# A complex recurrence on VectorE: real and imaginary parts in one operation, decay tables behind the gelu, 16 projection steps moved

## Chip, cores and metric

The kernel runs on one core of a Trainium2 chip. The metric is the time of one execution in microseconds; the profiled execution has its own time, and the profile shows its span from the first instruction to the last.

## What is computed

One layer of a hybrid encoder over two requests, 1024 and 256 tokens of width 1024, 1280 tokens together. An RMS norm is followed by one projection to 5120 columns. Branch A is a bidirectional diagonal state-space recurrence (S5) with a gelu and a gated linear unit; branch B is differential attention with rotary positions. Both are gated, projected, merged under sigmoid gates, projected once more, added to the input and normed. The change touches the recurrence, which is in the reference:

```python
bu = jnp.einsum('ngpc,lgc->nlgp', B_bar, us.astype(jnp.complex64))
a = jnp.broadcast_to(A_bar[:, None], bu.shape)
_, h_f = lax.associative_scan(_scan_combine, (a[0], bu[0]), axis=0)
_, h_b = lax.associative_scan(_scan_combine, (a[1], bu[1]), axis=0, reverse=True)
y = jnp.einsum('gcp,lgp->lgc', C_c[0], h_f) + jnp.einsum('gcp,lgp->lgc', C_c[1], h_b)
```

A_bar and bu are complex; 32 groups of 16 channels have 64 states each, in two directions.

## The kernel before

Time is cut into strands of eight tokens (T = 8), so that a scan runs over J = 160 columns per group (128 of the long request, 32 of the short one). Within a strand the work is done by matrices prepared ahead. The state is rotated by a unit complex factor per column (the table `tb`, real and imaginary), so that the recurrence left over has a real decay: the same decay `rt` for the real and the imaginary part. Partitions 0 to 63 carry the forward direction, 64 to 127 the backward one.

The 32 groups go in eight blocks of four (NB = 4), 640 columns a block. A block b passes three functions (lines 788 to 852):

- `in_mm`: ScalarE writes the decay table `rt` (four activations at line 793, one a group, two buffers). For each half block of two groups TensorE makes the real and the imaginary input products in PSUM (`pr_`, `pi_`, lines 799 and 800). VectorE multiplies them with `tb`: four products of 320 columns (lines 805 to 808), into `bm`, `t1` and `t2`. GpSimd adds `t1` and subtracts `t2` (lines 809 and 810). `t1` and `t2` have one buffer each.
- `scan`: for the real and then the imaginary part a forward scan on partitions 0 to 63 (line 820), a backward one on 64 to 127 (line 821), both over 640 columns, and two memsets (824, 825). Then six VectorE operations of 640 columns rotate back (lines 830 to 835), into `e`.
- `out_mm`: 24 TensorE matmuls (lines 848 to 850) from `e` and the inputs, and a gelu on ScalarE for each half block (line 851).

TensorE's order in this stage is written by hand: PE and SP follow the program. Between the recurrence's matmuls stand projection steps (`fill`). A step is three matmuls (lines 729 to 731) of 424 or 432 columns; eight steps are a chunk, which ScalarE evicts (line 735) and stores by its own DMA queue (line 736); three chunks are a tile of 128 output columns, 24 steps. For each tile a weight is loaded by ScalarE's queue (line 218), cast by ScalarE (line 239) and its remainder taken on GpSimd (line 240, `wl`: the weight split) once a tile two before it is done. There are 24 tiles, 576 steps. S_PRE = 22 steps stand ahead of `in_mm(0)`, S_LEAD = 10 behind it, and in each of the eight blocks S_MID = 13 between `in_mm(b + 1)` and `out_mm(b)` and S_END = 4 behind `out_mm(b)`: 168 in all. Attention takes 288 by its own counts. The 120 left are put in by `fill(1000)` (line 1168) behind the first gated unit and attention's gating (`glu_stage`, `ya_stage`), ahead of the merge: its matmuls (`xb`, line 1081 to 1083) take weights that are cast and split at lines 1074 and 1075. There, and on VectorE, GpSimd and ScalarE everywhere, the order is chosen by a scheduler that models the run at build time.

The loop that sets the order (lines 867 to 889) issues for block b: the loads for later blocks, `scan(b)`, `in_mm(b + 1)`, S_MID steps, `out_mm(b)`, S_END steps.

Of the kernel before, what the change touches and what calls it, by code (L numbers as in the profile page):

```python
# [39 lines left out]
S_PRE, S_LEAD, S_MID, S_END = 22, 10, 13, 4  # L40
# [86 lines left out]
def kernel(  # L127
# [624 lines left out]
    with ExitStack() as p2:  # L752
# [34 lines left out]

        def in_mm(b, tb, wb):
            q, gb = b // 2, (b % 2) * NB
            u = U[q]  # L790
            rt = sp_.tile([128, NB, J], F32, tag="rt", name="rt", bufs=2)
            for g in range(NB):
                A.activation(rt[:, g], rmask, AF.Copy, scale=r8[:, b * NB + g:b * NB + g + 1])
            bm = sp_.tile([128, 2, NB, J], F32, tag="bm", name="bm", bufs=2)
            for h in range(NB // 2):
                pr_ = ps_b.tile([128, 2, J], F32, tag="pr", name="pr")
                pi_ = ps_b.tile([128, 2, J], F32, tag="pi", name="pi")
                for g in range(2):
                    PE.matmul(pr_[:, g], wb[:, 0, 2 * h + g], u[:, gb + 2 * h + g], start=True, stop=True)
                    PE.matmul(pi_[:, g], wb[:, 1, 2 * h + g], u[:, gb + 2 * h + g], start=True, stop=True)  # L800
                t1 = sp_.tile([128, 2, J], F32, tag="t1", name="t1")
                t2 = sp_.tile([128, 2, J], F32, tag="t2", name="t2")
                gsl = slice(2 * h, 2 * h + 2)
                tr_, ti_ = tb[:, 0, gsl], tb[:, 1, gsl]
                V.tensor_tensor(bm[:, 0, gsl], pr_, tr_, op=ALU.mult)
                V.tensor_tensor(t1, pi_, ti_, op=ALU.mult)
                V.tensor_tensor(t2, pr_, ti_, op=ALU.mult)
                V.tensor_tensor(bm[:, 1, gsl], pi_, tr_, op=ALU.mult)
                G.tensor_tensor(bm[:, 0, gsl], bm[:, 0, gsl], t1, op=ALU.add)
                G.tensor_tensor(bm[:, 1, gsl], bm[:, 1, gsl], t2, op=ALU.subtract)  # L810
            return rt, bm

        def scan(b, tb, rt, bm):
            n = NB * J
            z = []
            for r in range(2):
                zz = sp_.tile([128, n + 2], F32, tag=f"z{r}", name=f"z{r}")
                rf = rt.rearrange("p g j -> p (g j)")
                bf = bm[:, r].rearrange("p g j -> p (g j)")
# [3 lines left out]
                zv = zz[:, 1:n + 1].rearrange("p (g j) -> p g j", j=J)  # L823
                V.memset(zv[0:64, :, 0:J:JL], 0.0)
                V.memset(zv[64:128, :, JL - 1:J:JS], 0.0)
                z.append(zv)
            e = sp_.tile([128, 2, NB, J], F32, tag="e", name="e", bufs=2)
            f1 = sp_.tile([128, NB, J], F32, tag="f1", name="f1")
            f2 = sp_.tile([128, NB, J], F32, tag="f2", name="f2")
            V.tensor_tensor(e[:, 0], z[0], tb[:, 0], op=ALU.mult)  # L830
            V.tensor_tensor(f1, z[1], tb[:, 1], op=ALU.mult)
# [26 lines left out]
        with tc.manual_schedule(engines={mybir.EngineType.PE, mybir.EngineType.SP}):  # L858
# [415 lines left out]
```

## Time and profile before

| what | value |
|---|---|
| median of 3 runs | 1108.75 us (1108.33 to 1112.75) |
| profiled execution | 1107.61 us |
| its span | 1105.5 us |
| TensorE matmul busy | 1062.7 us, 96% |
| VectorE busy | 765.3 us, 69% |
| ScalarE busy | 462.9 us, 42% |
| GpSimd busy | 325.3 us, 29% |
| mean granted TensorE clock | 0.992 |

Busy time is what the profile records between an instruction's start and end. Matmul records overlap, so a TensorE that is called busy can still take more work. The chain of work that ended last is followed back from the last instruction, at each step to what released it. In the rows, a number in brackets at the end of a timeline row is the engine's idle time just before and what ended it.

### The profile page before, as it was taken

How to read it: one execution, taken by the hardware profiler on the slowest of the kernel's cores; microseconds unless marked ns; L12 is line 12 of the kernel's file. 1: busy time of each engine (PE TensorE's matmuls, PEld its weight loads, DVE VectorE, ACT ScalarE, POOL GpSimd, SP SyncE). 2: the span in 40 equal slices, each digit the busy share in tenths (PEclk: the TensorE clock that was granted, in tenths of full speed). 3: DMA queues.
4: the chain of work that ended last, by engine and by line, in shares of the span. 5: the costliest groups of instructions: out<-in, count | busy, mean ns of one | idle time of the engine just before them, and what ended most of it. 6: DMA issues, size and time to landing. Idle time of an engine off the chain costs nothing.

```text
span 1105.5 us, 17989 instructions
## 1 busy us (share of the span) xinstructions
PE 1062.7 (96%) x6479; PEld 983.2 (89%) x6479; DVE 765.3 (69%) x1534; ACT 462.9 (42%) x929; POOL 325.3 (29%) x435
## 2 busy tenths in 40 slices
PE   8989999999989899999999999999999999999997
PEld 6868877888979888899999999899999999998997
DVE  7996847877599997577767876876443676666434
ACT  5543322322321212555654664554543455543332
POOL 1619887011234232212312222221240003520032
PEclk9999999999999999999999999999999999999999
DMA  8656454445767667417317316302646974568122
GB/s 244 160 162 218 155 165 164 157 134 192 252 196 225 176 186 202 139 36 198 111 36 208 114 58 174 119 25 80 204 124 197 300 223 112 174 202 259 48 58 95
DMA packets 186154, 173.59 MB, mean 157 GB/s; under 512 B 32721, under 2 KB 161745, under 8 KB 186066
## 3 DMA queue, kind: packets, MB, share of 16 engines
q1 hardware_dynamic: 150736, 144.13, 44.2%
q10 hardware_dynamic: 35330, 28.32, 8.1%
q8 instruction: 51, 0.84, 0.3%
q14 instruction: 37, 0.30, 0.1%
HBM read 113.71 MB, written 58.69 MB: 156 GB/s over the span
## 4 chain that ended last, share of the span: by engine, by line
PE 48%; DVE 19%; DMA 7%; ACT 3%; issue 3%; POOL 2%; SPq 0%; POOLq 0%; ACTq 0%; DVEq 0%
PE mm L729 5%; PE mm L730 5%; PE mm L731 5%; PE xb L1081 3%; PE xb L1082 3%; PE xb L1083 3%; DVE z L821 2%; DVE z L820 2%; PE S L947 2%; PE tr L972 2%; PE S L949 2%; DMA yt<-ya_d 2%; PE tr L1214 2%; PE tr L1215 2%; PE tr L1216 2%
## 5 line engine op out<-in xcount | busy, mean ns | idle before, releaser
L729 PE MATMUL mm<-hTh,wh 128*128 128x424 f32 (+1 forms) x576 | 211.9, 368 | 5.2 <-ACT zo L735 5.0
L731 PE MATMUL mm<-hTh,wl 128*128 128x424 f32 (+1 forms) x576 | 205.8, 357 | 0.0
L730 PE MATMUL mm<-hTl,wh 128*128 128x424 f32 (+1 forms) x576 | 205.4, 357 | 0.0
L729 PEld LDWEIGHTS mm<-hTh,wh 128*128 128x128 f32 x576 | 108.8, 189 | 11.4 <-ACT zo L735 7.0
L730 PEld LDWEIGHTS mm<-hTl,wh 128*128 128x128 f32 x576 | 109.0, 189 | 4.5
L731 PEld LDWEIGHTS mm<-hTh,wl 128*128 128x128 f32 x576 | 108.7, 189 | 3.3
L951 DVE TENSOR_REDUCE mx<-S 128x1 f32<-128x1024 f32 (+1 forms) x80 | 84.3, 1058 | 37.8 <-PE S L949 37.5
L955 ACT ACTIVATE p<-S,mx 128x1024 f32<-128x1024 f32 (+1 forms) x80 | 79.2, 993 | 58.9 <-DVE mx L952 47.1
L240 POOL TENSOR_TENSOR wl<-wst,wh 128x1024 fp32r<-128x1024 f32 x24 | 64.8, 2701 | 127.8 <-ACT wh L239 79.2
L962 POOL TENSOR_SCALAR p<-p,rs 128x1024 f32<-128x1024 f32 (+1 forms) x40 | 41.5, 1037 | 201.3 <-DVE rs L960 195.3
L1214 PE MATMUL tr<-wqh,mh 128*128 128x256 f32 x320 | 89.7, 281 | 2.0 <-DVE o L1218 2.0
L1215 PE MATMUL tr<-wql,mh 128*128 128x256 f32 x320 | 89.2, 279 | 0.0
L1216 PE MATMUL tr<-wqh,ml 128*128 128x256 f32 x320 | 88.9, 279 | 0.0
L246 PE MATMUL mm<-hTh,wh 128*128 128x512 f32 (+1 forms) x192 | 75.0, 391 | 0.0
L247 PE MATMUL mm<-hTl,wh 128*128 128x512 f32 (+1 forms) x192 | 72.6, 378 | 0.0
L248 PE MATMUL mm<-hTh,wl 128*128 128x512 f32 (+1 forms) x192 | 72.5, 378 | 0.0
L1214 PEld LDWEIGHTS tr<-wqh,mh 128*128 128x128 f32 x320 | 60.1, 188 | 2.9 <-DVE o L1218 2.9
L1215 PEld LDWEIGHTS tr<-wql,mh 128*128 128x128 f32 x320 | 60.1, 188 | 0.0
L1216 PEld LDWEIGHTS tr<-wqh,ml 128*128 128x128 f32 x320 | 60.0, 188 | 0.0
L735 ACT COPY zo<-mm 128x424 f32<-128x424 f32 (+1 forms) x72 | 37.0, 514 | 53.0 <-PE mm L731 27.1
L1221 POOL TENSOR_TENSOR o<-o,finB 128x256 f32<-128x256 f32 x30 | 28.2, 943 | 103.5 <-ACT jk L1220 103.5
L976 DVE TENSOR_TENSOR wTl<-tr,wTh 128x512 fp32r<-128x512 f32 (+1 forms) x72 | 46.7, 656 | 14.0 <-ACT wTh L975 12.9
(396 smaller groups left out, 2827.1 us busy)
## 6 DMA issues: line engine op xcount, KB each, us to landing
wst<-in_w_in_dram ACTq DMA_DIRECT2D x24, 512.0 KB, 4.2
wst<-in_w_in_dram SPq DMA_DIRECT2D x16, 512.0 KB, 5.4
wst<-in_w_branch_dram SPq DMA_DIRECT2D x32, 256.0 KB, 4.8
wqs<-in_w_out_dram SPq DMA_DIRECT2D x16, 512.0 KB, 4.1
tt_d<-tt SPq DMA_DIRECT2D x16, 320.0 KB, 3.1
tb<-tt_d SPq DMA_DIRECT2D x8, 640.0 KB, 5.0
zt<-gs_d SPq DMA_DIRECT2D x16, 320.0 KB, 3.9
x<-in_x_sample_dram SPq DMA_DIRECT2D x8, 512.0 KB, 5.5
```

Of the source, the lines that this page charges most:

```text
L240: e.tensor_tensor(lv, st, hv, op=ALU.subtract)
L246: PE.matmul(ps[:, :n], wh[:, k, :], hTh[:, k, c0:c0 + n], start=(k == 0), stop=False)
L247: PE.matmul(ps[:, :n], wh[:, k, :], hTl[:, k, c0:c0 + n], start=False, stop=False)
L248: PE.matmul(ps[:, :n], wl[:, k, :], hTh[:, k, c0:c0 + n], start=False, stop=(k == KD - 1))
L729: PE.matmul(ps[:, :n], wh[:, k, :], hTh[:, k, c0:c0 + n], start=(k == 0), stop=False)
L730: PE.matmul(ps[:, :n], wh[:, k, :], hTl[:, k, c0:c0 + n], start=False, stop=False)
L731: PE.matmul(ps[:, :n], wl[:, k, :], hTh[:, k, c0:c0 + n], start=False, stop=(k == KD - 1))
L951: V.tensor_reduce(mx, S[:, :nk], axis=AX.X, op=ALU.max)
L955: A.activation(p[:, :nk], S[:, :nk], AF.Exp, bias=mx, scale=1.0 / math.sqrt(HD), accum_out=sm[:, t:t + 1])
L1214: PE.matmul(ps[:, :256], mh[:, k, ts_], oh_[:, k], start=(k == 0), stop=False)
L1215: PE.matmul(ps[:, :256], mh[:, k, ts_], ol_[:, k], start=False, stop=False)
L1216: PE.matmul(ps[:, :256], ml[:, k, ts_], oh_[:, k], start=False, stop=(k == 7))
```

## The change

It does four things. Real and imaginary parts share one operation: the PSUM products of a half block lie in one tile `pp_`, one VectorE product with the imaginary table writes `t` and one with the real table writes `bm`, each over 640 columns; the forward and the backward scan each run over 1280 columns, with a decay table that holds the same decay twice; two memsets clear the edges; two products of 1280 columns and an add and a subtract of 640 rotate back. The decay table is made by a function of its own, two blocks ahead of its scan, and placed behind the gelu of block b with `after(sig)`, which queues it behind that instruction on ScalarE; the first two are made ahead of `in_mm(0)`. S_LEAD goes from 10 to 18 and S_MID from 13 to 14: 8 + 8 steps come out of the 120 behind attention.

```diff
-S_PRE, S_LEAD, S_MID, S_END = 22, 10, 13, 4
+S_PRE, S_LEAD, S_MID, S_END = 22, 18, 14, 4
...
+        def decay(b):
+            rt = sp_.tile([128, 2, NB, J], F32, tag="rt", name="rt", bufs=2)
+            for g in range(NB):
+                A.activation(rt[:, :, g], bc(rmask, 1, 2), AF.Copy, scale=r8[:, b * NB + g:b * NB + g + 1])
+            return rt.rearrange("p r g j -> p (r g j)")
+
         def in_mm(b, tb, wb):
...
-            rt = sp_.tile([128, NB, J], F32, tag="rt", name="rt", bufs=2)
-            for g in range(NB):
-                A.activation(rt[:, g], rmask, AF.Copy, scale=r8[:, b * NB + g:b * NB + g + 1])
...
-                pr_ = ps_b.tile([128, 2, J], F32, tag="pr", name="pr")
-                pi_ = ps_b.tile([128, 2, J], F32, tag="pi", name="pi")
+                pp_ = ps_b.tile([128, 2, 512], F32, tag="pp", name="pp")
...
-                V.tensor_tensor(bm[:, 0, gsl], pr_, tr_, op=ALU.mult)
-                V.tensor_tensor(t1, pi_, ti_, op=ALU.mult)
-                V.tensor_tensor(t2, pr_, ti_, op=ALU.mult)
-                V.tensor_tensor(bm[:, 1, gsl], pi_, tr_, op=ALU.mult)
-                G.tensor_tensor(bm[:, 0, gsl], bm[:, 0, gsl], t1, op=ALU.add)
-                G.tensor_tensor(bm[:, 1, gsl], bm[:, 1, gsl], t2, op=ALU.subtract)
+                t = sp_.tile([128, 2, n], F32, tag="t", name="t")
+                V.tensor_tensor(t, pp_[:, :, :n], ti_, op=ALU.mult)
+                V.tensor_tensor(bm[:, :, sl_], pp_[:, :, :n], tr_, op=ALU.mult)
+                G.tensor_tensor(bm[:, 0, sl_], bm[:, 0, sl_], t[:, 1], op=ALU.add)
+                G.tensor_tensor(bm[:, 1, sl_], bm[:, 1, sl_], t[:, 0], op=ALU.subtract)
...
         def scan(b, tb, rt, bm):
-            n = NB * J
...
-                V.tensor_tensor_scan(zz[0:64, 2:n + 2], rf[0:64], bf[0:64], 0.0, ALU.mult, ALU.add)
-                V.tensor_tensor_scan(zz[64:128, 0:n][:, ::-1], rf[64:128, ::-1], bf[64:128, ::-1], 0.0,
-                                     ALU.mult, ALU.add)
...
+            n = 2 * NB * J
+            zz = sp_.tile([128, n + 2], F32, tag="z", name="z")
+            bf = bm.rearrange("p r n -> p (r n)")
+            V.tensor_tensor_scan(zz[0:64, 2:n + 2], rt[0:64], bf[0:64], 0.0, ALU.mult, ALU.add)
+            V.tensor_tensor_scan(zz[64:128, 0:n][:, ::-1], rt[64:128, ::-1], bf[64:128, ::-1], 0.0, ALU.mult, ALU.add)
...
-            V.tensor_tensor(e[:, 0], z[0], tb[:, 0], op=ALU.mult)
-            V.tensor_tensor(f1, z[1], tb[:, 1], op=ALU.mult)
-            V.tensor_tensor(e[:, 0], e[:, 0], f1, op=ALU.subtract)
-            V.tensor_tensor(e[:, 1], z[1], tb[:, 0], op=ALU.mult)
-            V.tensor_tensor(f2, z[0], tb[:, 1], op=ALU.mult)
-            V.tensor_tensor(e[:, 1], e[:, 1], f2, op=ALU.add)
-            return e
+            V.tensor_tensor(e, z, tr_, op=ALU.mult)
+            V.tensor_tensor(f, z, ti_, op=ALU.mult)
+            V.tensor_tensor(e[:, 0], e[:, 0], f[:, 1], op=ALU.subtract)
+            V.tensor_tensor(e[:, 1], e[:, 1], f[:, 0], op=ALU.add)
+            return e.rearrange("p r (g j) -> p r g j", j=J)
...
+            rts = [decay(0), decay(1)]
             cur = in_mm(0, tbs[0], wbs.pop(0))
...
                 sig = out_mm(b, wcs.pop(b), e)
+                if b + 2 < NBLK:
+                    with after(sig):
+                        rts.append(decay(b + 2))
                 fill(S_END)
```

In the new code `tr_` and `ti_` are the tables broadcast over the two parts, n is 320 in `in_mm`, and `sl_` is the half block's 320 columns.

## Rows read from the trace of the kernel before

**Rows 1.** The page, chain that ended last: shares of the span by engine.

```profile
PE 48%; DVE 19%; DMA 7%; ACT 3%; issue 3%; POOL 2%; SPq 0%; POOLq 0%; ACTq 0%; DVEq 0%
```

**Rows 2.** Recurrence stage: length, busy PE, PEld, DVE, ACT, POOL (count), clock, DMA share, GB/s.

```profile
290.00:441.00 151.00, 139.63 (x792) 134.11 (x791) 130.84 (x176) 33.46 (x76) 46.73 (x38) 0.98 0.71 206
```

**Rows 3.** VectorE's waits in that stage: waiter, releaser, total us, times, longest.

```profile
DVE z L820 <- POOL bm L809: 2.3, 7, 0.3
DVE t L806 <- POOL bm L809: 1.8, 7, 0.3
```

**Rows 4.** From the first product of block 0 to the end of block 7.

```profile
298.90:436.90 138.00, 126.68 (x715) 121.28 (x713) 130.84 (x176) 28.36 (x62) 46.73 (x38) 0.98 0.70 199
```

**Rows 5.** TensorE's timeline: output matmuls of blocks 0, 1, 2 and 7; an eviction wait.

```profile
319.93 0.83 PE L848 MATMUL tr<-e,wcm 128*128 128x160 f32 x2 [4.55 <-DVE e L832]
...
337.35 0.43 PE L848 MATMUL tr<-e,wcm 128*128 128x160 f32 x2
...
352.68 0.44 PE L848 MATMUL tr<-e,wcm 128*128 128x160 f32 x2
...
365.62 0.46 PE L729 MATMUL mm<-hTh,wh 128*128 128x424 f32 x1 [2.11 <-ACT zo L735]
...
436.26 0.51 PE L848 MATMUL tr<-e,wcm 128*128 128x160 f32 x2 [1.29 <-issue]
```

**Rows 6.** VectorE's timeline: first part of block 3 and its first two scans.

```profile
350.42 0.49 DVE L805 TENSOR_TENSOR bm<-pr,tb 128x320 f32<-128x320 f32 x1
350.82 0.48 DVE L807 TENSOR_TENSOR t<-pr,tb 128x320 f32<-128x320 f32 x1
351.22 0.48 DVE L806 TENSOR_TENSOR t<-pi,tb 128x320 f32<-128x320 f32 x1
...
352.01 0.48 DVE L805 TENSOR_TENSOR bm<-pr,tb 128x320 f32<-128x320 f32 x1
352.75 0.49 DVE L806 TENSOR_TENSOR t<-pi,tb 128x320 f32<-128x320 f32 x1 [0.26 <-POOL bm L809]
...
354.39 2.13 DVE L820 TENSOR_TENSOR_SCAN z<-rt,bm 64x640 f32<-64x640 f32 x1 [0.33 <-POOL bm L809]
356.56 3.51 DVE L821 TENSOR_TENSOR_SCAN z<-rt,bm 64x640 f32<-64x640 f32 x1
```

**Rows 7.** VectorE's timeline: scans and combination of block 2.

```profile
338.77 2.13 DVE L820 TENSOR_TENSOR_SCAN z<-rt,bm 64x640 f32<-64x640 f32 x1 [0.33 <-POOL bm L809]
...
343.96 1.49 DVE L821 TENSOR_TENSOR_SCAN z<-rt,bm 64x640 f32<-64x640 f32 x1
...
346.00 0.83 DVE L830 TENSOR_TENSOR e<-z,tb 128x640 f32<-128x640 f32 x1
346.74 0.82 DVE L834 TENSOR_TENSOR f<-z,tb 128x640 f32<-128x640 f32 x1
```

**Rows 8.** Weight splits on GpSimd, 298.8 to 437: busy us, mean ns, idle before; one split.

```profile
L240 POOL TENSOR_TENSOR wl<-wst,wh 128x1024 fp32r<-128x1024 f32 x6 | 18.3, 3053 | 20.5 <-ACT wh L239 20.5
...
355.15 3.57 POOL L240 TENSOR_TENSOR wl<-wst,wh 128x1024 fp32r<-128x1024 f32 x1
```

**Rows 9.** GpSimd's timeline: add and subtract of block 3's first half.

```profile
351.84 0.88 POOL L809 TENSOR_TENSOR bm<-bm,t 128x320 f32<-128x320 f32 x1 [12.29 <-DVE t L806]
352.69 0.86 POOL L810 TENSOR_TENSOR bm<-bm,t 128x320 f32<-128x320 f32 x1
```

**Rows 10.** Decay tables on ScalarE, 298.8 to 437: busy us, mean ns, idle before.

```profile
L793 ACT ACTIVATE rt<-rmask,r 128x160 f32<-128x160 f32 x24 | 8.3, 418 | 54.4 <-DVE z L821 54.4
```

**Rows 11.** TensorE's and VectorE's timelines where projection steps end and the merge begins.

```profile
842.01 0.42 PE L1081 MATMUL xb<-ysh,wh 128*128 128x320 f32 x1
...
842.56 0.35 PE L729 MATMUL mm<-hTh,wh 128*128 128x424 f32 x1
...
851.84 0.31 PE L1083 MATMUL xb<-ysh,wl 128*128 128x320 f32 x1
...
841.99 1.23 DVE L1075 TENSOR_TENSOR wl<-wst,wh 128x1024 fp32r<-128x1024 f32 x1
```

More of the change, by code (lines that the diff above doesn't have):

```diff
@@ L790, in in_mm @@
             u = U[q]
-            rt = sp_.tile([128, NB, J], F32, tag="rt", name="rt", bufs=2)
-            for g in range(NB):
-                A.activation(rt[:, g], rmask, AF.Copy, scale=r8[:, b * NB + g:b * NB + g + 1])
-            bm = sp_.tile([128, 2, NB, J], F32, tag="bm", name="bm", bufs=2)
+            bm = sp_.tile([128, 2, NB * J], F32, tag="bm", name="bm", bufs=2)
             for h in range(NB // 2):
-                pr_ = ps_b.tile([128, 2, J], F32, tag="pr", name="pr")
-                pi_ = ps_b.tile([128, 2, J], F32, tag="pi", name="pi")
+                pp_ = ps_b.tile([128, 2, 512], F32, tag="pp", name="pp")
@@ L798, in in_mm @@
                 for g in range(2):
[L799 to L804, printed above, removed]
-                V.tensor_tensor(bm[:, 0, gsl], pr_, tr_, op=ALU.mult)
@@ new lines, in in_mm @@
+                    for r in range(2):
+                        PE.matmul(pp_[:, r, g * J:g * J + J], wb[:, r, 2 * h + g], u[:, gb + 2 * h + g],
+                                  start=True, stop=True)
+                n = 2 * J
+                sl_ = slice(h * n, h * n + n)
+                tr_, ti_ = (bc(tb[:, r, 2 * h:2 * h + 2].rearrange("p g j -> p (g j)"), 1, 2) for r in range(2))
+                t = sp_.tile([128, 2, n], F32, tag="t", name="t")
+                V.tensor_tensor(t, pp_[:, :, :n], ti_, op=ALU.mult)
@@ new lines, in in_mm @@
+                V.tensor_tensor(bm[:, :, sl_], pp_[:, :, :n], tr_, op=ALU.mult)
+                G.tensor_tensor(bm[:, 0, sl_], bm[:, 0, sl_], t[:, 1], op=ALU.add)
+                G.tensor_tensor(bm[:, 1, sl_], bm[:, 1, sl_], t[:, 0], op=ALU.subtract)
+            return bm
+        def scan(b, tb, rt, bm):
+            n = 2 * NB * J
[3 more added lines that the diff above has]
+            V.tensor_tensor_scan(zz[64:128, 0:n][:, ::-1], rt[64:128, ::-1], bf[64:128, ::-1], 0.0, ALU.mult, ALU.add)
+            zv = zz[:, 1:n + 1].rearrange("p (g j) -> p g j", j=J)
+            V.memset(zv[0:64, :, 0:J:JL], 0.0)
+            V.memset(zv[64:128, :, JL - 1:J:JS], 0.0)
+            z = zz[:, 1:n + 1].rearrange("p (r n) -> p r n", r=2)
+            e = sp_.tile([128, 2, NB * J], F32, tag="e", name="e", bufs=2)
+            f = sp_.tile([128, 2, NB * J], F32, tag="f", name="f")
+            tr_, ti_ = (bc(tb[:, r].rearrange("p g j -> p (g j)"), 1, 2) for r in range(2))
+            V.tensor_tensor(e, z, tr_, op=ALU.mult)
[3 more added lines that the diff above has]
+            return e.rearrange("p r (g j) -> p r g j", j=J)
@@ L880 @@
                     store_y(q - 1)
-                e = scan(b, tbs.pop(b), *cur)
+                e = scan(b, tbs.pop(b), rts.pop(0), cur)
                 if b + 1 < NBLK:
```

13 lines of the change are left out of this document (removed).

## The prediction

> **What bounds the kernel now.** I read the busy shares by stage first, then the waits inside the recurrence stage, then one block of that stage instruction by instruction. Over the whole program the chain of work that ended last lies mostly on TensorE, with VectorE second [rows 1]. In the recurrence stage it is VectorE: 130.8 of 151 us busy [rows 2], and all that VectorE waits for there, after one load at the start, is GpSimd, seven times before a scan and seven times before a product, 4.1 us together [rows 3]. The stage lasts 138.0 us from the first product of block 0 to the end of block 7 [rows 4].
>
> TensorE runs beside it and is the engine that waits: 4.55 us before the output matmuls of block 0, about 2 us where an eviction was late, 1.29 us before the outputs of block 7 [rows 5]. So what the stage costs is read from VectorE, and the projection steps are what TensorE does meanwhile.
>
> A block without a disturbance has three parts. From its first product to its first scan 3.97 us: 350.42 to 354.39 [rows 6]. From there to the first product after the memsets 7.23 us: 338.77 to 346.00. From there to the next block's first product 4.42 us: 346.00 to 350.42 [rows 6, 7]. Sum 15.62 us, times eight 125.0 us. The other 13.0 us of the 138.0 belong to the six weight splits that GpSimd runs in that time [rows 8], 2.17 us each. How a split costs VectorE is seen in the second scan of the block: 3.51 us in place of 1.49 [rows 6, 7].
>
> **The merged operations, step by step.** Products of 320 columns start 0.40 us apart (350.42, 350.82) [rows 6], operations of 640 columns 0.74 us apart (346.00, 346.74) [rows 7]: about 0.06 us fixed and 1.06 ns a column. Merging saves 0.06 us for each operation that goes. It also changes who waits.
>
> *First part.* Per half block two products of 640 columns replace four of 320. GpSimd's add and subtract now both read the one buffer t, which has one copy, so the second half's t waits for both; before, t1 waited for the add alone. With the first product at 0, bm of the first half starts at 0.74 and ends at 1.56. GpSimd starts 0.14 us after its last input (351.70 to 351.84), its two operations start 0.85 us apart and the second takes 0.86 [rows 6, 9]: it is done at 3.41. Meanwhile bm of the second half runs, as now the second half's first product is put ahead of the waiting one (352.01 before 352.75) [rows 6]. The second t runs from 3.44 to 4.26, GpSimd's second pair from 4.40 to 6.11, the scan starts at 6.14. Before it needed only the add; now it needs the subtract too. That is 2.17 us more than 3.97. If t goes ahead of bm in the second half, 0.74 more.
>
> *Scans.* Nothing in the trace scans 1280 columns. Two scans of 640 take 2.98 us; if a scan has the fixed 0.14 us by which a recorded operation of 640 columns (0.82) exceeds its columns, one of 1280 takes 2.84. I bound it by 2.70 and 2.98 and take 2.84, which is nearest to how the other operations behave. Two of them, two memsets in place of four and the gaps give 6.0 us, against 7.23. Half of that gain is that the first scan, 2.13 us beside GpSimd's subtract [rows 7], now starts when GpSimd is done.
>
> *Combination.* Two products of 1280 columns at 1.42, a subtract and an add of 640 at 0.74: 4.32, and about 0.1 because the subtract reads what the operation just ahead of it wrote. 4.42, as now.
>
> Sum: 6.14 + 6.0 + 4.42 = 16.56 us a block, 0.94 more than 15.62; eight blocks, 7.5 us more.
>
> **The splits.** A weight tile lasts 24 projection steps, and its successor's split follows its last step. From the first step to block 7's outputs there were 22 + 10 + 8 x 13 + 7 x 4 = 164 steps, six full tiles; now there are 180, seven. One more split at 2.17 us; as VectorE now sits waiting for a fifth of a block, a split falls partly in that time, so seven at about 2.0 against six at 2.17: 1.0 us more. Bounds: no more than now, and 3.05 for the one more (the mean split's whole time on GpSimd) [rows 8].
>
> **The decay tables.** Their activations no longer stand on ScalarE ahead of the scan that frees their buffer, where they held the queue for 54.4 us [rows 10], evictions and weight casts behind them included. The price of that was TensorE waiting about 2 us for an eviction [rows 5]. TensorE had that time to spare, since VectorE set the end, so I cost its end at nothing. Each activation is now twice as wide, four a block; 0.42 us each becomes at most 0.84, so at most 3.4 us a block on an engine busy 33 of 151 us [rows 2, 10]. Behind the gelu of block b they have a block's time until the scan of b + 2. Where the gelu waits for TensorE's outputs, evictions queue behind it as now; the cover is the second projection bank. The eight at the start end some microseconds ahead of the first scan. SP's queue and GpSimd's are passed by nothing of this.
>
> **The 16 steps.** Each step is three matmuls; the 16 steps between 842.56 and 851.84 took 9.28 us, 0.58 a step [rows 11]. In the recurrence stage they are covered: TensorE reaches the outputs of block 0 at 315.4 now (319.93 less 4.55 [rows 5]), with nine steps more at 320.6, while block 0 ends on VectorE at 298.9 + 16.6 + 2.2 = 317.7. Later a block takes TensorE 15.33 us (337.35 to 352.68 [rows 5]) and a step more makes 15.9, under VectorE's 16.56 plus splits. The two evictions, two stores and two thirds of a weight load, cast and split that go with the steps move along; ScalarE and its queue have room, and the split is counted above. At the other end, the steps leave the stretch behind attention. There exactly 16 steps stand after the first merge matmul could start (842.01), and that matmul's third term lacks only the weight split, ready at 843.22 [rows 11]. Without the 16 steps TensorE waits about 0.7 us for it: a gain of 8.6 us, bounds 7 and 9.3.
>
> **Sum.** +7.5 + 1.0 - 8.6 = -0.1 us on the profiled execution's 1107.61, so no change; the median of the three runs is 1108.75, 1.1 above it. I forecast **1108.6 us**. The bounds (scans 2.2 us either way, t ahead of bm 5.9 up, splits 2, tail 1.6 up or 0.7 down) make the forecast's own range about 1103.5 to 1115.
>
> **Rivals.**
>
> *The number of operations decides.* A block goes from 22 VectorE operations to 12. If the waits for GpSimd are hidden, because the scheduler puts the next block's first products among the combination of this one (as it did once, between the scans of blocks 0 and 1), a block is 10 x 0.06 us shorter, 4.8 us over the stage, and TensorE at 15.9 a block keeps up: 1108.75 - 4.8 - 8.6 = 1095.3. For it speaks that the two products of a half need only TensorE's inputs. Against it: in a steady block the products now come strictly behind the combination, and t2 comes ahead of t1 (350.82, 351.22 [rows 6]), the order in which TensorE delivers, so the scheduler believed VectorE to be waiting for TensorE there and had no reason to hoist; eight more steps ahead make TensorE later still in its eyes. This is what the Trainium skill says, VectorE: DVE Perf Modes, Rules for kernel authors, where chained operations are to be reduced in number and semaphores are said to matter little. By that rule the stage shrinks; the rows say that a hand-off to GpSimd and back costs 0.14 + 1.71 us and an operation 0.06, so I give it the smaller chance: 0.22.
>
> *GpSimd's order.* GpSimd runs in order, and a weight split may stand ahead of the adds for which VectorE now waits four times a block. Then VectorE pays the whole split, up to 3.57 us [rows 8], not 2.17; with seven splits 1.4 x 7 = 9.8 us, 1118.4. It decides against the kernel from 0.8 us a split on (5.5 / 7). For it: GpSimd already waited 20.5 us with a split at its head for a cast [rows 8]. Against: none of the products' waits in the trace was longer than 0.3 us [rows 3]. 0.13.
>
> *The tail gives nothing back.* If the chain through the gated unit and attention's gating ends later than now, TensorE waits for it where the 16 steps stood, the gain of 8.6 shrinks and the time is up to 1115, inside the range: 0.05.
>
> **Chances.** Forecast 0.60, operations 0.22, GpSimd's order 0.13, tail 0.05. A measurement of this kernel tells about 0.5%, 5.5 us, from no change. Faster: the operations rival and 0.05 of the forecast, 0.27. Slower: GpSimd's order, and 0.09 from the forecast's and the tail's upper ends, 0.22. Same: 0.51. The range 1096 to 1115 leaves out half of the first rival and most of the second.
>
> **What the changed profile would show.** First part of a block near 6.1 us, with VectorE waiting for GpSimd's subtract twice, about 1.2 and 1.9 us; scans near 2.84; period 16.6, or 18.7 with a split; the stage 146 us long; no wait of TensorE for an eviction, but for e in most blocks; no projection step behind the first merge matmul. A first part under 5 us, or products among the combination, would prove the forecast wrong on the fast side; a split ahead of an add with VectorE waiting over 3 us, on the slow side.

## The result and the profile after

The changed kernel takes **1115.86 us** (median of 16 runs, 1110.88 to 1117.53) against 1108.65 for the kernel before on the same chip: ratio 1.0059, 95% interval 1.0045 to 1.0073. It is slower by about 0.6%. The forecast was 1108.6 us, the range 1096 to 1115; the time lies 0.9 us above the range. The profiled execution took 1115.66 us (span 1113.8), 8.4 us of span more than the one before.

I cut the span at four places that both traces have: VectorE's first product of block 0; the end of its last operation of block 7; the start of the last norm matmul of attention; the start of the last projection step's last matmul. "Attention stage" below is from the second to the third. "Units" is the distance from the first to the last unit's reciprocal in attention, which lies inside it and leaves both edges out.

| stage, us | before | after | difference |
|---|---|---|---|
| ahead of the first product | 298.9 | 298.4 | -0.5 |
| recurrence | 138.0 | 146.7 | +8.7 |
| attention stage | 343.6 | 351.7 | +8.1 |
| to the last projection step | 71.1 | 62.2 | -9.0 |
| to the end | 253.8 | 254.9 | +1.1 |

The forecast had +8.5 for the second line and -8.6 for the fourth. It had no line for attention, and nearly the whole error of its sum lies there: 8.1 us, of which 7.6 are in the units (306.8 and 314.4).

**Recurrence.** The windows view, from the first product to the end of block 7, answers to [rows 4]: busy TensorE, weight loads, VectorE, ScalarE, GpSimd with counts, clock, DMA share, GB/s.

```profile
298.36:445.11 146.75, 135.83 (x766) 129.51 (x764) 115.84 (x96) 34.60 (x66) 45.54 (x39) 0.99 0.70 199
```

VectorE has 96 instructions instead of 176 and 115.8 us of work instead of 130.8, and the stage is longer. Its waits, against [rows 3]:

```profile
DVE z L818 <- POOL bm L811: 16.3, 8, 2.5
DVE t L808 <- DMA tb<-tt_d: 10.3, 1, 10.3
DVE t L808 <- PE tr L845: 7.4, 4, 1.9
DVE t L808 <- POOL bm L811: 5.3, 4, 1.9
```

Where 4.1 us of waiting for GpSimd stood, there are 29.0: 16.3 before the scans, and 12.7 before the second half's t. The third line names TensorE, but GpSimd's subtract is what came last: in block 3 it ends at 355.61, and t starts at 355.64. GpSimd's timeline there:

```profile
354.75 0.86 POOL L811 TENSOR_TENSOR bm<-bm,t 128x320 f32<-128x320 f32 x1
```

VectorE's timeline of block 3, in which no split falls, against [rows 6, 7]:

```profile
352.23 0.82 DVE L808 TENSOR_TENSOR t<-pp,tb 128x640 f32<-128x640 f32 x1
352.97 0.81 DVE L809 TENSOR_TENSOR bm<-pp,tb 128x640 f32<-128x640 f32 x1
355.64 0.82 DVE L808 TENSOR_TENSOR t<-pp,tb 128x640 f32<-128x640 f32 x1 [1.86 <-PE tr L845]
356.38 0.81 DVE L809 TENSOR_TENSOR bm<-pp,tb 128x640 f32<-128x640 f32 x1
359.00 2.82 DVE L818 TENSOR_TENSOR_SCAN z<-rt,bm 64x1280 f32<-64x1280 f32 x1 [1.80 <-POOL bm L811]
...
364.99 1.49 DVE L827 TENSOR_TENSOR e<-z,tb 128x1280 f32<-128x1280 f32 x1
...
369.40 0.82 DVE L808 TENSOR_TENSOR t<-pp,tb 128x640 f32<-128x640 f32 x1
...
393.96 4.98 DVE L818 TENSOR_TENSOR_SCAN z<-rt,bm 64x1280 f32<-64x1280 f32 x1 [1.80 <-POOL bm L811]
```

First part 6.77 us (352.23 to 359.00), scans 5.99, combination 4.41: 17.17 a block. In the second half t stands ahead of bm and holds it back. The last line is a scan beside a weight split: 4.98 instead of 2.82. The splits on GpSimd, against [rows 8]:

```profile
L240 POOL TENSOR_TENSOR wl<-wst,wh 128x1024 fp32r<-128x1024 f32 x7 | 16.7, 2389 | 2.6 <-ACT wh L239 2.6
```

Seven, as forecast. Eight blocks of 17.17 are 137.4. Four of the splits lie beside a scan, which takes 2.0 to 2.2 us longer; three stand between GpSimd's two pairs of a block, and the scan behind them waits about 2.4 us instead of 1.8. That is 10.4 us in all, 1.5 a split. In two blocks (1 and 2) the scheduler put the first half's products among the combination of the block before, and this took some 1.1 us off: the first three blocks last 53.9 us (298.36 to 352.23), where three of 17.17 and their splits would make 55.0. VectorE's timeline where blocks 1 and 2 meet, and the scan of block 4, which waits for a pair behind a split:

```profile
331.84 0.82 DVE L808 TENSOR_TENSOR t<-pp,tb 128x640 f32<-128x640 f32 x1
...
333.31 0.81 DVE L829 TENSOR_TENSOR e<-e,f 128x640 f32<-128x640 f32 x1
...
336.31 0.82 DVE L808 TENSOR_TENSOR t<-pp,tb 128x640 f32<-128x640 f32 x1 [0.77 <-POOL bm L811]
...
376.80 2.82 DVE L818 TENSOR_TENSOR_SCAN z<-rt,bm 64x1280 f32<-64x1280 f32 x1 [2.44 <-POOL bm L811]
```

**Attention.** The windows view over the units (columns as above), first of the kernel before.

```profile
450.60:757.43 306.83, 299.87 (x1767) 279.03 (x1767) 226.76 (x418) 167.75 (x343) 70.20 (x50) 1.00 0.36 105
```

The same view of the changed kernel:

```profile
459.75:774.15 314.40, 303.90 (x1765) 281.15 (x1765) 234.72 (x418) 168.97 (x345) 70.32 (x51) 0.99 0.35 101
```

TensorE's work is the same to two matmul records. It stands idle 10.5 us instead of 7.0, and its matmuls take 4.0 us longer. Before, its longest waits in the units were for the exponentials on ScalarE (who waits, for whom, total, times, longest):

```profile
PE S L947 <- ACT p L955: 4.3, 5, 1.4
```

After:

```profile
PE tr L971 <- DVE mx L951: 6.8, 3, 2.3
...
PE mm L729 <- ACT zo L735: 1.8, 4, 0.4
PE tr L983 <- DVE mx L951: 1.7, 3, 0.6
```

Three waits of 2.3 us, at the start of a head each. The first of them, on GpSimd's timeline:

```profile
539.66 2.51 POOL L240 TENSOR_TENSOR wl<-wst,wh 128x1024 fp32r<-128x1024 f32 x1 [16.56 <-ACT wh L239]
542.15 1.56 POOL L961 TENSOR_SCALAR p<-p,rs 128x1024 f32<-128x1024 f32 x1
```

On VectorE's timeline:

```profile
539.95 2.77 DVE L1016 SCALAR_TENSOR_TENSOR ya<-ya,rr 128x512 f32<-128x512 f32 x1
542.64 0.15 DVE L960 TENSOR_TENSOR rs<-rs,nlam 128x1 f32<-128x1 f32 x1
542.75 1.50 DVE L1017 TENSOR_TENSOR ya<-ya 128x512 f32<-128x512 f32 x1
544.17 1.21 DVE L950 TENSOR_REDUCE mx<-S 128x1 f32<-128x1024 f32 x1
545.31 0.41 DVE L996 TENSOR_TENSOR ya<-ya 128x256 f32<-128x256 f32 x1
545.64 1.27 DVE L962 SCALAR_TENSOR_TENSOR p<-p,rs,p 128x1024 f32<-128x1024 f32 x1
```

And on TensorE's:

```profile
546.97 1.09 PE L971 MATMUL tr<-ident,p 128*128 128x128 f32 x8 [2.26 <-DVE mx L951]
```

A weight split starts on GpSimd while VectorE begins a norm operation of the pair just finished (L1016). That operation takes 2.77 us where its neighbour L1015 took 0.68. Behind it in VectorE's order stand the factors rs, the row maxima and the combination of p (L962), and TensorE's transposes (L971) wait for that p. (Their row names mx L951, which ends 0.01 us after they began; p is done at 546.91.) VectorE has no idle time from 539.22 on, and GpSimd's own share of p (L961), held back behind the split, is done at 543.71, so it is VectorE's time that counts.

A split beside a norm product is not enough, though. The kernel before has such meetings too. VectorE's timeline of it, the first product of a norm, which takes 0.68 us undisturbed:

```profile
501.15 2.87 DVE L1015 TENSOR_TENSOR ya<-ya,rr 128x512 f32<-128x512 f32 x1
```

It happens again at 662.58, and two combinations of p take 3.20 us instead of 1.28; yet behind these four TensorE waits 1.0 us at most at a time. At the start of a head, where the change put the meeting, TensorE had run out of work at 544.71, 2.26 us ahead of its transposes.

The clock follows in two of the three cases: it was granted 0.57 and 0.65 of full speed in the 4 us behind the waits at 629.98 and 714.52, so part of each stretch ran at 1.2 GHz and not 2.4. That is 1.7 and 1.4 us of full-speed time lost, an estimate from the granted clock, and so most of the 4.0 us by which the matmuls took longer. Behind the wait at 546.97 it stayed at 1.00. The windows view of the three stretches:

```profile
547.00:551.00 4.00, 4.00 (x24) 3.77 (x25) 3.95 (x8) 3.79 (x7) 1.13 (x1) 1.00 0.35 95
...
630.00:634.00 4.00, 4.00 (x16) 3.82 (x17) 3.95 (x8) 3.27 (x6) 1.12 (x1) 0.57 0.38 102
...
714.50:718.50 4.00, 3.98 (x18) 3.77 (x19) 3.95 (x9) 3.27 (x6) 1.12 (x1) 0.65 0.35 97
```

**The tail.** TensorE's timeline, against [rows 11]:

```profile
849.42 0.31 PE L1080 MATMUL xb<-ysh,wh 128*128 128x320 f32 x1
...
849.86 0.35 PE L729 MATMUL mm<-hTh,wh 128*128 128x424 f32 x1
...
858.95 0.36 PE L731 MATMUL mm<-hTh,wl 128*128 128x424 f32 x1
859.14 0.31 PE L1082 MATMUL xb<-ysh,wl 128*128 128x320 f32 x1
```

Sixteen steps stand behind the first merge matmul, as before. The 16 that left did so from the stretch ahead of it.

### The profile page after: what moved, and what is told of

The parts are those of the page before. It is cut to its first block, busy times and chain, and to the rows that moved or that the text cites. A ratio compares the mean times of both kernels' runs of the same rounds, so it can differ in the third digit from the quotient of the medians.

```text
span 1113.8 us, 17906 instructions
## 1 busy us (share of the span) xinstructions
PE 1067.5 (96%) x6479; PEld 986.6 (89%) x6479; DVE 759.0 (68%) x1454; ACT 468.7 (42%) x929; POOL 321.2 (29%) x435
## 4 chain that ended last, share of the span: by engine, by line
PE 51%; DVE 15%; DMA 7%; issue 4%; POOL 3%; ACT 2%; SPq 0%; POOLq 0%; ACTq 0%; DVEq 0%
PE mm L729 7%; PE mm L730 7%; PE mm L731 7%; DVE z L818 2%; PE tr L971 2%; PE S L946 2%; PE xb L1080 2%; PE S L948 2%; PE xb L1081 2%; PE xb L1082 2%; DVE z L819 2%; PE mm L247 2%; PE mm L246 2%; PE mm L248 2%; PE tr L1213 2%
## 5 line engine op out<-in xcount | busy, mean ns | idle before, releaser
L961 POOL TENSOR_SCALAR p<-p,rs 128x1024 f32<-128x1024 f32 (+1 forms) x40 | 42.6, 1064 | 209.1 <-DVE rs L959 186.7
L240 POOL TENSOR_TENSOR wl<-wst,wh 128x1024 fp32r<-128x1024 f32 x24 | 58.0, 2418 | 115.2 <-ACT wh L239 95.7
```

The lines of the kernel that those rows point to most:

```text
L240: e.tensor_tensor(lv, st, hv, op=ALU.subtract)
```

## The experiments

Theory P: what costs 8 us in attention is the place at which the weight tiles change there. A tile is 24 steps and a head takes 72, so whatever place the tile's change has in one head it has in all four; 168 and 192 steps ahead of attention are whole numbers of tiles, 184 are 16 steps into one. Rival M: the merged operations cause it, by the later end of the recurrence or another order of work behind it. Theory G, for the recurrence: the price is the hand-off to GpSimd. All results in one table. The stages (us) are those of one profiled execution, which can lie some microseconds off the median; the ratio is to the kernel before on the same chip.

| run | steps | recurrence | attention stage | units | to last step | to end | median, ratio (95%) |
|---|---|---|---|---|---|---|---|
| e1_fill_only | 184 | 139.7 | 351.5 | 314.6 | 62.2 | 255.9 | 1108.28, 0.9995 (0.9979 to 1.0011) |
| e2_merge_only | 168 | 144.1 | 344.3 | 306.0 | 72.3 | 253.4 | 1117.25, 1.0066 (1.0046 to 1.0087) |
| e3_rt_only | 168 | 137.9 | 343.6 | 306.4 | 71.1 | 254.1 | 1106.51, 0.9991 (0.9970 to 1.0013) |
| e4_merge_192 | 192 | 151.2 | 344.2 | 306.4 | 56.7 | 262.2 | 1111.12, 1.0022 (1.0011 to 1.0033) |
| f1_t_two | 184 | 138.8 | 350.3 | 314.7 | 62.2 | 257.9 | 1108.57, 0.9982 (0.9962 to 1.0002) |
| f2_v_adds_168 | 168 | 131.6 | 346.2 | 309.4 | 72.3 | 254.7 | 1104.18, 0.9934 (0.9916 to 0.9953) |
| f3_small_184 | 184 | 146.5 | 339.5 | 303.9 | 62.4 | 257.3 | 1106.34, one run |
| f4_small_168 | 168 | 144.0 | 336.9 | 299.5 | 74.8 | 255.9 | 1109.67, one run |
| g1_bm_first | 184 | 144.3 | 350.1 | 314.4 | 62.2 | 257.8 | 1111.79, 1.0031 (1.0016 to 1.0047) |
| g2_fill_176 | 176 | 136.7 | 359.5 | 313.4 | 66.8 | 255.5 | 1113.72, 1.0057 (1.0036 to 1.0077) |
| g3_v_adds_176 | 176 | 131.1 | 346.1 | 308.9 | 66.8 | 255.5 | 1098.70, 0.9908 (0.9886 to 0.9930) |
| g4_v_adds_192 | 192 | 132.5 | 346.3 | 306.9 | 56.7 | 258.5 | 1093.61, 0.9880 (0.9856 to 0.9903) |
| h1_vsplit_184 | 184 | 146.7 | 341.9 | 304.8 | 61.8 | 255.1 | 1105.47, 0.9974 (0.9958 to 0.9990) |
| h2_vsplit_before | 168 | 138.0 | 339.1 | 307.0 | 71.8 | 256.1 | 1102.30, 0.9952 (0.9933 to 0.9971) |
| h3_vsplit_adds_192 | 192 | 132.5 | 338.9 | 303.8 | 57.6 | 258.4 | 1086.22, 0.9808 (0.9787 to 0.9830) |

### Which part costs what: e1, e2, e3, e4

e1_fill_only: the kernel before, steps alone.

```diff
-S_PRE, S_LEAD, S_MID, S_END = 22, 10, 13, 4
+S_PRE, S_LEAD, S_MID, S_END = 22, 18, 14, 4
```

> The kernel before with S_LEAD 18 and S_MID 14 alone: 184 projection steps in the recurrence, nothing merged, decay tables where they were. Theory P (phase): attention takes three weight tiles a head (72 steps), so a count that is no multiple of 24 shifts casts, splits and evictions against attention's units in every head; attention (first scores to the end of its outputs) goes from 344 us to about 350, the stretch behind it loses 6.5 us, the recurrence has one more split (+2 us): total within 3 us of before. Rival M (the merged order is what lengthens attention): attention stays at 344 and the total falls by 5 to 8 us.

The recurrence is 1.7 us longer than before, attention 351.5 and 314.6, as in the changed kernel, though nothing is merged. The 16 steps alone bring the tail's 9.0 us and lose 7.9 of them in attention: ratio 0.9995. P holds, M falls.

e2_merge_only: the changed kernel, steps as before.

```diff
-S_PRE, S_LEAD, S_MID, S_END = 22, 18, 14, 4
+S_PRE, S_LEAD, S_MID, S_END = 22, 10, 13, 4
```

> The changed kernel with S_LEAD 10 and S_MID 13 back: 168 steps, merged operations and decay tables behind the gelu kept. Theory P: first product to the end of block 7 about 145 us (138 before, 146.7 in the changed kernel, one split less), attention back at about 344 us, the tail as before: total 6 to 8 us above before, about the changed kernel's time. Rival M: attention about 350 us as in the changed kernel, total 12 us or more above before.

Recurrence 6.1 us longer than before, attention within 0.8 us of before; by the medians 0.66% slower. So by the medians the merged operations cost what the whole change costs, and the steps bring nothing. The profiled execution took 1112.01 us, the shortest of the six; where the 5 us up to their median lie is not in its trace.

e3_rt_only: the kernel before with the decay tables two blocks ahead, behind the gelu.

```diff
+        def decay(b):
...
+            rts = [decay(0), decay(1)]
...
+                    with after(sig):
+                        rts.append(decay(b + 2))
```

> The kernel before with the decay tables alone put behind the gelu, 160 columns wide as before. Theory W (VectorE sets the recurrence's end): ScalarE's waits of 54 us go, TensorE's waits for evictions too, and the total stays within 2 us of before. Rival: ScalarE's late evictions cost time after all, and the total falls by 3 us or more.

No stage of the table moves by more than 0.3 us, ratio 0.9991 with 1 inside its interval: nothing, as the forecast costed it.

e4_merge_192: the changed kernel with S_LEAD 26.

```diff
-S_PRE, S_LEAD, S_MID, S_END = 22, 18, 14, 4
+S_PRE, S_LEAD, S_MID, S_END = 22, 26, 14, 4
```

> The changed kernel with S_LEAD 26: 192 steps, again a multiple of 24. Theory P: recurrence 147 to 149 us, attention back at about 344 us, the tail shorter than before by 6 to 9 us: total about 1108 to 1112. Rival M: attention about 350 us, total 1114 to 1118. If it is the number of steps left behind attention, and not the phase, that lengthens attention, it is 350 us or more here.

Attention is back at 344.2 and 306.4 with eight steps more than the change moved: it is not the number that costs. Against the changed kernel the tail gives 5.5 us more, but 7.3 are lost behind the last step (262.2), and the recurrence takes 4.5 more, 151.2 where 147 to 149 were expected. Why was not pursued.

### The recurrence: f1, g1, f2

f1_t_two: the changed kernel, two buffers for t.

```diff
-                t = sp_.tile([128, 2, n], F32, tag="t", name="t")
+                t = sp_.tile([128, 2, n], F32, tag="t", name="t", bufs=2)
```

> The changed kernel with two buffers for t instead of one; nothing else. Theory G (in the recurrence the price is the hand-off to GpSimd: the second half's t waits for GpSimd's subtract of the first half, idle 1.86 us in block 3 of the changed kernel): with a second buffer the four products of a block run 0.74 us apart, GpSimd's two pairs run back to back, and the scan starts about 5.2 us after the first product instead of 6.77. A block falls from 17.2 to about 15.6 us, which is at or under what TensorE needs with 18 steps (15.9); the recurrence from its first product to the end of block 7 takes 134 to 139 us instead of 146.8. Rival W (the wide operations themselves cost more than the narrow ones did, by the tables broadcast over two parts or by the PSUM tile's stride): the first part stays above 6 us and the recurrence at 145 to 148. Theory P (a place in the cycle of 24 projection steps decides the attention stage) expects the attention stage as in the changed kernel, 351 to 352 us, in either case, since 184 steps still stand ahead of it. Total: G and P 1104 to 1109; W 1115 to 1117.

Recurrence 138.8, at the upper end of what G gave; all waits of t for GpSimd are gone; the units stay at 314.7. W, that the wide operations themselves cost more, falls. One buffer cost 8 us. VectorE still waits for GpSimd before each scan, 19.9 us in all, and in two blocks the weight split stood between GpSimd's two pairs, the "GpSimd's order" rival in small: 4.4 us instead of 2.07. VectorE's timeline of f1 in one of them:

```profile
365.85 0.82 DVE L808 TENSOR_TENSOR t<-pp,tb 128x640 f32<-128x640 f32 x1
...
373.27 2.82 DVE L818 TENSOR_TENSOR_SCAN z<-rt,bm 64x1280 f32<-64x1280 f32 x1 [4.41 <-POOL bm L811]
```

g1_bm_first: the changed kernel, the products in the other order.

```diff
-                V.tensor_tensor(t, pp_[:, :, :n], ti_, op=ALU.mult)
                 V.tensor_tensor(bm[:, :, sl_], pp_[:, :, :n], tr_, op=ALU.mult)
+                V.tensor_tensor(t, pp_[:, :, :n], ti_, op=ALU.mult)
```

> The changed kernel with its two input products in the other order: bm first, then t; 184 steps. It is the order on which the forecast's first part of 6.14 us rested. Theory G (hand-off): the second half's bm runs while GpSimd works on the first half, only t waits; first part of a steady block 6.1 to 6.2 us instead of 6.77, and as two blocks of the changed kernel had their first half put among the combination already, the recurrence falls from 146.8 to 141 to 144 us; attention stage 350 to 352; total 1110 to 1114. Rival (VectorE's order in the second half is not what is waited for, GpSimd's two pairs set the scan's start in either order): recurrence 146 to 148, total 1115 to 1117.

VectorE's timeline of g1, first part of a block:

```profile
385.03 0.82 DVE L808 TENSOR_TENSOR bm<-pp,tb 128x640 f32<-128x640 f32 x1
385.76 0.82 DVE L809 TENSOR_TENSOR t<-pp,tb 128x640 f32<-128x640 f32 x1
386.50 0.81 DVE L808 TENSOR_TENSOR bm<-pp,tb 128x640 f32<-128x640 f32 x1
388.44 0.82 DVE L809 TENSOR_TENSOR t<-pp,tb 128x640 f32<-128x640 f32 x1 [1.14 <-POOL bm L811]
391.09 4.97 DVE L818 TENSOR_TENSOR_SCAN z<-rt,bm 64x1280 f32<-64x1280 f32 x1 [1.82 <-POOL bm L811]
```

First part 6.06 us (385.03 to 391.09), against 6.14 in the forecast: its sum was right for the order that it assumed. The recurrence falls by 2.5 us to 144.3, just above the 141 to 144 expected, and by less than eight times the 0.71 us of a first part: a split between GpSimd's pairs cost 1.4 us there (a scan's wait of 3.2 for 1.8, in two blocks) and 0.6 in the changed kernel. The total is 1111.79, inside what G gave and below the rival's.

f2_v_adds_168: add and subtract on VectorE over the whole block, steps as before.

```diff
+            t = sp_.tile([128, 2, NB * J], F32, tag="t", name="t")
...
-                G.tensor_tensor(bm[:, 0, sl_], bm[:, 0, sl_], t[:, 1], op=ALU.add)
-                G.tensor_tensor(bm[:, 1, sl_], bm[:, 1, sl_], t[:, 0], op=ALU.subtract)
+            V.tensor_tensor(bm[:, 0], bm[:, 0], t[:, 1], op=ALU.add)
+            V.tensor_tensor(bm[:, 1], bm[:, 1], t[:, 0], op=ALU.subtract)
```

> The changed kernel with the add and the subtract of the input products on VectorE, one of each over the whole block of 640 columns, and the counts of steps as before (10 and 13, 168 steps). No operation of the recurrence is left on GpSimd but the weight split. Theory G (hand-off to GpSimd is the price): first part of a block about 6 x 0.74 = 4.4 us plus 0.1 for a dependent start, 4.5 instead of 6.77; block about 15.0 us; TensorE with 17 steps needs 15.33 and is the bound or level with it; recurrence 130 to 136 us; attention stage 343 to 345 (168 steps); behind it about 71 until the last projection step. Total 1101 to 1107. Rival (VectorE's own work is the price, and GpSimd took part of it): two operations more on VectorE, 1.5 us a block, recurrence 144 + 12 = 156 us or near it, total 1122 to 1128.

VectorE's timeline of f2, first part of a block:

```profile
382.22 0.82 DVE L808 TENSOR_TENSOR t<-pp,tb 128x640 f32<-128x640 f32 x1
...
386.00 0.82 DVE L811 TENSOR_TENSOR bm<-bm,t 128x640 f32<-128x640 f32 x1
386.93 2.82 DVE L818 TENSOR_TENSOR_SCAN z<-rt,bm 64x1280 f32<-64x1280 f32 x1
```

First part 4.71 us with two operations more on VectorE; recurrence 131.6 us, 6.4 less than before. With the hand-off gone, the merged operations do pay. An undisturbed block takes 15.10 us (350.04 to 365.14) for 15.62 before, near the 0.6 us a block of the rival "number of operations"; but VectorE also has two operations more and no wait for GpSimd left, so this run does not tell the saving per operation from the rest. Attention (346.2) came out 1 us above the range expected.

### Attention: f3, f4, g2, h1, h2

f3_small_184 and f4_small_168: the changed kernel with 184 and with 168 steps, and a weight split of one eighth from the tenth tile on; the other seven eighths of those remainders are left out.

```diff
-        e.tensor_tensor(lv, st, hv, op=ALU.subtract)
+        e.tensor_tensor(lv[:, :part], st[:, :part], hv[:, :part], op=ALU.subtract)
...
-                    PE.matmul(ps[:, :n], wl[:, k, :], hTh[:, k, c0:c0 + n], start=False, stop=(k == KD - 1))
+                    PE.matmul(ps[:, :n], wl[:, 0 if i >= 9 else k, :], hTh[:, k, c0:c0 + n], start=False, stop=(k == KD - 1))
...
-                        ws.append(w_split(w_stage(tiles[i + 2][1], A), G))
+                        ws.append(w_split(w_stage(tiles[i + 2][1], A), G, part=1 if i + 2 >= 9 else KD))
```

> The changed kernel, in which GpSimd's weight split covers one eighth of the columns for the tiles from the tenth on, whose splits fall in the attention stage or behind it; the third term of those tiles multiplies by that eighth each time, so the other seven eighths of the weights' remainders are left out there. The number of matmuls, casts, loads and evictions is the same. Theory P (with 184 steps ahead, each head's weight split falls beside the first pair's norm on VectorE, slows it from 0.69 to 2.77 us, and what stands behind makes TensorE wait some 2.3 us a head): the attention stage falls from 351.7 to 342 to 345 us, and the waits of 2.3 us at the head's start go. Rival E (the place of the evictions, casts or loads in the attention units costs the 8 us, not the split): the attention stage stays at 350 to 352. The recurrence stays at about 147.

> The changed kernel with 10 and 13 steps as before (168 ahead of attention) and the same small split for the tiles from the tenth on, so the remainders of seven eighths of those weights are left out. It is the measure for the run with 184 steps: theory P expects the two attention stages within 2 us of each other (here 341 to 344.5; with the whole split it was 344.3 at this count), rival E expects 343 to 345 here and 350 to 352 there.

Attention stage 339.5 and 336.9, both lower than expected: 12.2 us less with 184 steps, 7.4 less with 168. The gap between the counts falls from 7.4 to 2.6 us, where P gave 2 at most, and in the units from 8.4 to 4.4. E, that evictions, casts or loads cost it, falls; P carries half to two thirds of the gap. The four waits for evictions (1.8 us) stay with 184 steps and are absent with 168.

g2_fill_176: the kernel before, S_MID 14 and S_LEAD 10.

```diff
-S_PRE, S_LEAD, S_MID, S_END = 22, 10, 13, 4
+S_PRE, S_LEAD, S_MID, S_END = 22, 10, 14, 4
```

> The kernel before with S_MID 14 and S_LEAD 10: 176 steps ahead of attention, 8 more than before and 8 fewer than with the change, a place of 8 in the cycle of 24 where before it was 0 and with the change 16. Recurrence 138 to 139.5; from attention's last norm to the last step 71.1 - 4.6 = 66.5. Theory P (the place in the cycle decides, by whether a weight split falls beside a pair's norm): the attention stage is one of two kinds, 343 to 346 if the splits miss the norms, 350 to 352 if they meet them, and not between; total 1103 to 1106 or 1110 to 1113. Rival D (attention loses about 0.5 us for each step moved ahead of it): 347.6, total 1108.

A miss for both theories in the stage: 359.5. The units take 313.4, of the costly kind, but TensorE also waits 11.02 us, until 428.02, for a load of keys: the first scores stood in its order ahead of block 6's outputs, and the keys had not landed. Block 7's outputs start at 444.8, 10.5 us behind VectorE's last operation. The profiled execution is also the longest of the six, 1118.31 for a median of 1113.72. So the place in the cycle isn't the only thing that the number of steps moves.

h1_vsplit_184: the changed kernel, the splits from the tenth tile on made by VectorE; h2_vsplit_before: the same edit in the kernel before.

```diff
-                        ws.append(w_split(w_stage(tiles[i + 2][1], A), G))
+                        ws.append(w_split(w_stage(tiles[i + 2][1], A), V if i + 2 >= 9 else G))
```

> The changed kernel (184 steps) with the weight splits of the tiles from the tenth on, which fall in the attention stage, done by VectorE instead of GpSimd; nothing left out. A split of this size took VectorE 1.23 us where the kernel does it there already; on GpSimd it took 2.4 to 2.5 and slowed the VectorE operation beside it by 2.1 (2.77 instead of 0.69 us). Measure: from the first to the last unit's reciprocal in attention, 314.4 us in the changed kernel, 306.8 in the kernel before, 303.9 with one eighth of the split. Theory P' (what costs is GpSimd's split beside VectorE's work): 304 to 308, the three waits of TensorE of 2.3 us shrink to 1.2 or go, total 1106 to 1110. Rival (the place in the cycle costs through the order of VectorE's work, whichever engine splits): 311 to 315, total 1113 to 1118.

> The same change of engine for the splits in the kernel before (168 steps). The attention measure was 306.8 us there, and 299.5 with one eighth of the split in the changed kernel at this count of steps. Theory P': 301 to 306, so that the two counts differ by 4 us or less where they differed by 7.6; total 1103 to 1108. Rival (VectorE's time is worth more than GpSimd's slowdown): 307 to 312, total 1109 to 1114.

h1's timeline at the start of the second head, the place of the 2.77 us above:

```profile
537.15 1.22 DVE L240 TENSOR_TENSOR wl<-wst,wh 128x1024 fp32r<-128x1024 f32 x1
538.28 0.69 DVE L1016 SCALAR_TENSOR_TENSOR ya<-ya,rr 128x512 f32<-128x512 f32 x1
```

TensorE's waits over h1's units:

```profile
PE tr L971 <- DVE p L962: 2.9, 3, 1.0
PE mm L729 <- ACT zo L735: 1.8, 4, 0.4
```

The split is at the same place, 1.22 us on VectorE, and the norm operation beside it is back at 0.69. The three waits shrink from 2.3 to 1.0, the units from 314.4 to 304.8, the kernel to 1105.47, a ratio of 0.9974 where the change had 1.0059. So it is GpSimd's split beside VectorE's work that cost, most of it: of the 1.3 us by which a wait shrinks, 0.3 may come from another order on VectorE (L996 now stands behind L962). h2 gains 4.5 us in the attention stage and its total is slightly better than expected; its units (307.0) miss the 301 to 306, but hold 1789 matmuls instead of 1767, so they are not like for like. The gap between 184 and 168 steps is now 2.8 us of stage (341.9 and 339.1), where it was 8.1.

### Versions that beat both kernels: g3, g4, h3

g3_v_adds_176 and g4_v_adds_192 are f2 with other counts; h3_vsplit_adds_192 is g4 with the splits of h1.

```diff
-S_PRE, S_LEAD, S_MID, S_END = 22, 10, 13, 4
+S_PRE, S_LEAD, S_MID, S_END = 22, 10, 14, 4
```

for g3, and for g4 and h3

```diff
+S_PRE, S_LEAD, S_MID, S_END = 22, 18, 15, 4
```

> The changed kernel with the add and the subtract of the input products on VectorE over the whole block, and 176 steps (10 and 14). With 168 steps the recurrence took 131.6 us. Now TensorE has 18 steps a block, 15.9 us, over VectorE's 15.0: recurrence 132 to 136. Attention stage as in the kernel before with 176 steps, plus up to 2 us. Behind it 4.6 us less than the 72.3 with 168 steps. Total, if the attention stage is 343 to 347: 1099 to 1103; if it is 350 to 352: 1106 to 1109.

> The same with 192 steps (18 and 15), a whole number of cycles. TensorE has 19 steps a block, 16.5 us, and is the bound: recurrence 135 to 141. Theory P: attention stage 343 to 347 again, since 192 is 8 x 24. Behind it 56 to 58 us to the last step, but from there to the end 8 us more than with 168 steps (262 instead of 254), as measured with 192 steps in the changed kernel. Total 1099 to 1106. Rival D (attention loses 0.5 us a step): attention 356, total 1112 or more.

> The fastest kernel so far (the changed recurrence with add and subtract on VectorE, 192 steps, 1093.6 us) with the same change of engine for the splits from the tenth tile on. Theory P': attention measure 301 to 306 instead of 306.9, total 1088 to 1093. Rival: 307 to 312, total 1094 to 1099.

With the recurrence shorter, steps can be moved until VectorE's and TensorE's time there meet. In g4 TensorE has no recorded wait between the first product and the end of block 7, and that stage takes 132.5 us, under the 135 expected; 192 steps are eight tiles, and the units take 306.9. D, a loss of 0.5 us in attention for each step moved, falls. g3 has three waits of 2 us in attention and takes 308.9, between P's two kinds. h3 adds the gain of h1: 1086.22 us, 1.9% under the kernel before. All three totals came out below what was expected of them, by 0.3 us (g3), 5.4 (g4) and 1.8 (h3).

## Why the prediction was wrong

**The bound.** Right: the recurrence is read from VectorE, and from VectorE's waits for GpSimd.

**The merged operations.** Size nearly right, by luck: errors of opposite sign. First part 6.14 forecast, 6.77 measured: the step "as now the second half's first product is put ahead of the waiting one" failed; t kept its place, and the alternative that the forecast named as its bound (0.74 more) came true, at 0.63. g1 shows that the other order gives 6.06. Eight blocks of 17.17 for 16.56 are 4.9 us up. The splits were sized at 2.0 us and cost 1.5: 10.4 for 14, 3.6 down. The products among the combination in two blocks, which the forecast took for a sign that it was wrong on the fast side, are 1.1 down. Scans (2.82 for 2.84, part 5.99 for 6.0) and combination (4.41 for 4.42) were right. Together +8.5 forecast, +8.7 measured.

**The decay tables.** Right: nothing (e3). In the recurrence TensorE's waits for evictions are down to one, of 1.3 us.

**The 16 steps.** The gain of 8.6 was right (9.0, and again in e1), the place wrong: I said that no step would stand behind the first merge matmul, and 16 do. So the 0.7 us of waiting that I took off came to nothing, and the 9.0 are nearly the whole time of 16 steps.

**The step that failed** is the sentence that the steps "are covered" in the recurrence and "leave the stretch behind attention". The sum went from the one stretch to the other and had no term for the 344 us between. There every tile change moved by 16 of 24 steps. I counted the split that comes to the recurrence, and not that the splits of attention come at another place. The price is 8 us in the attention stage: shown by e1 (the steps alone bring it) and by e2 and e4 (whole tiles don't). That the splits make it is shown for most of it: with the splits off GpSimd in both counts of steps (h1, h2) 2.8 of the 8.1 us are left. A row for it was in the trace: one split had turned a scan of 1.49 us into 3.51 [rows 6, 7], and splits ran all through attention too.

**The rivals.** "GpSimd's order" gave 1118.4, near the time by luck, and is not why: in the changed kernel a split that stood between two pairs cost about 0.6 us (a scan's wait of 2.44 in place of 1.80), three times. "The number of operations decides" failed by its own condition: products stood among the combination in two blocks of eight only, and the waits for GpSimd grew from 4.1 us to 29.0. The rule cited for it, the Trainium skill, VectorE: DVE Perf Modes, Rules for kernel authors, is for chained operations of VectorE. f2 agrees with it against the kernel before (14 operations a block for 22, 6.4 us less); against e2 (two operations more and no hand-off, 12.5 us less) a hand-off to another engine counted for more than the number. "The tail gives nothing back" did not happen.

**Open.** The 2.8 us left between 184 and 168 steps in the attention stage once the splits are off GpSimd; waits for evictions are 1.8 of them at most. Why 176 steps cost 313.4 in one kernel and 308.9 in another was not pursued.

## What to carry to other kernels

Filler work moved from one stage to another shifts the phase of everything that recurs with it (casts, splits, evictions) in all the stages between: count what recurs, and look at what it will stand beside there. Merging operations paid here when the second engine was out of the chain (f2), and hardly with two buffers (f1, 138.8 us, against e1, 139.7); where a second engine answers each of them through one buffer, count the round trips first. When a gain is missing, cut both traces at common landmarks: the stage that nobody touched may hold it.

## What the hardware showed that was not expected

- A GpSimd split of 2.4 to 2.5 us adds almost its whole length to one VectorE operation that reads two tables from SBUF: a scan of 1280 columns went from 2.82 to 4.98 us, a norm product of 512 from 0.69 to 2.77. The row maxima, which read PSUM, took their usual 1.22 us beside a split (at 485.91 and 487.67 in the changed kernel). The Trainium skill, SBUF — State Buffer, Who interferes with whom, says that a VectorE instruction with two inputs from SBUF contends with a GpSimd instruction that reads SBUF; these rows agree.
- VectorE makes the same split in 1.22 us, half the time. It can slow GpSimd in turn: at the start of three heads in h1 GpSimd's share of p, begun beside it, took 2.53 us instead of 1.13.
- After an idle of 2.26 us TensorE's clock was granted at 0.57 and 0.65 in the next 4 us twice, and at 1.00 once (behind the wait at 546.97), at the same place of a head.
